# State-space stage of a hybrid decoder block: result channels on the partitions instead of tokens

## The chip, the cores and the metric

The kernel runs on one core of a Trainium2 chip. The metric is the device time of one execution in microseconds (us); the median of several runs counts, and lower is better. TensorE (PE, with its weight loads as PEld), VectorE (DVE), ScalarE (ACT), GpSimd (POOL) and the DMA queues (SP issues most of them) each work through a list of instructions of their own, in order, and wait for each other through semaphores.

## The reference

One layer of a decoder trunk over 512 tokens of width 1024, in float32. One projection of the normalised input feeds three token mixers: a sparse attention (DSA), a second attention with compressed, selected and window keys (NSA), and a Mamba-2 state-space mixer (SSD). Gated, the three results go through an output projection and a feed-forward layer. What the change touches is the SSD mixer, in chunks of 128 tokens (c: chunk, g: group of 8 heads, h: head, p: one of 64 channels of a head):

```python
y_diag = jnp.einsum('bcijg,bcijgh,bcjgh,bcjghp->bcighp', cb, lmat, dtc, xs)
states = jnp.einsum('bcjgn,bcjgh,bcjghp->bcghpn', bm, decay_states * dtc, xs)
...
y_off = jnp.einsum('bcign,bcghpn,bcigh->bcighp', cm, h_in, jnp.exp(a_cum))
y = y_diag + y_off + xs * d_skip.reshape(SSD_GROUPS, SSD_HPG)[:, :, None]
y = y.reshape(bsz, seq, SSD_INNER)
y = rms_norm(y * jax.nn.silu(z.astype(jnp.float32)), norm_g)
```

`cb` is C times B transposed, `lmat` the lower-triangular decay between two tokens of a chunk, `h_in` the state carried into a chunk. `x`, `z`, B, C and the step sizes come from the projection, x, B and C after a causal convolution of width 4 and a silu.

## The kernel before, in words

**Two generators.** `main` runs the mixers one after the other: the DSA index and attention, then `ssd`, then the NSA attention. `filler` runs the dense work: all input projections, the gates (`do_mg`) and, in `branches`, the three branch projections, the output projection and the feed-forward layer. Each `yield` of `main` gives a number of nanoseconds, scaled by a ratio (R3 = 0.5 for `ssd`); `filler` is advanced until it has emitted as much. A scheduler then orders the instructions of each engine by its own estimate of when they are ready, with priorities, so the order on an engine is not the order of emission. Where `main` needs a projection it yields its name (`x0`, `z0`) and the filler is advanced until it is done; in `branches` the filler waits in turn for marks of the NSA attention (`nsa0`, `nsah`, `nsaq0`, `nsaq1`, `nsa`), since its branch is computed last, its final quarter of tokens in `b2`.

**Projections.** A product of two float32 operands of full precision is made of three products of halves (`mm3`, lines 455 to 457: hi·hi, hi·lo, lo·hi). `proj_tok` has tokens on the output partitions (the input stationary, weights moving) and `proj_ch` has channels there (weights stationary). Weights arrive as `wraw` by DMA on SP and are split into `whi` on ACT (line 172) and `wlo` on DVE or POOL (line 174).

**What feeds the stage.** `do_z` (line 721) projects z with `proj_tok`, makes silu(z) times two from a tanh (lines 724, 725) and stores it token by token in `xz_d`. `do_x` and `conv` (lines 771, 831) project x, B and C with `proj_ch`, run the convolution on DVE and the silu, transpose the result on PE (line 848) and store x token by token in `xz_d`, B and C in `bct_d`.

**The stage** (`ssd`, line 1262) has 16 units, one for each group g and chunk c, in the order (0,0), (1,0), (0,1), (1,1) and so on, then groups 2 and 3. `stage1` loads B, C (`bcx`, line 1273) and the running sums of the decay, broadcast to all partitions (`E`, line 1275), two units ahead; `load_xz` (line 1282) loads x and z. `stage2` makes C·B (`cbm`, line 1289), masks E on POOL (line 1290), takes exponentials on ACT (line 1293), multiplies with `cbm` on DVE (line 1300) and scales x on POOL by the step (`xt`, line 1295), by step and decay (`xw`, line 1298) and by D (line 1302). `stage3` multiplies C with the carried state (line 1311, output `po`), scales it by exp(a_cum) on DVE (line 1313), adds D·x on POOL (line 1314), makes the chunk's state (line 1318) and updates the carried one (lines 1323, 1324). Then come eight y products, one per head (line 1330): E stationary, 64 columns of `xt` moving, tokens on the output partitions. The sum is multiplied with z (lines 1334, 1335), squared and summed by row on ACT (line 1336), transposed by four PE transposes (line 1341, emitted in the unit after), scaled by the gain of the norm in four ACT evictions (line 1344) and stored in `yc_d` (line 1345). At the end the row sums give the norm's factor (`rst`, line 1378), stored in `rs_d`. `load_y` (line 811) loads `yc_d` for the branch and splits it into halves.

Of the kernel before, what the change touches and what calls it, by code (L numbers as in the profile page):

```python
# [41 lines left out]
def build_kernel(ctx, tc, A, out):  # L42
# [35 lines left out]
    xz_d = scratch("xz_d", [2 * S, 2048])  # L78
# [136 lines left out]
    def plan_order(item):  # L215
# [5 lines left out]
        elif kind == "z":  # L221
            P["z", k] = plan_tok(w_in, D_IN, [(C_Z + k * 512, 512)])
# [95 lines left out]
    dskip = cp.tile([128, 32], F32, name="dskip")  # L318
    CL = {}

    def const_load():
# [20 lines left out]
        put(dskip, A["ssd_d"], 32)  # L342
# [348 lines left out]
    def filler():  # L691
# [119 lines left out]
    def load_y(yp, br, kk):  # L811
# [8 lines left out]
        act.activation(h_, yr, AF.Copy)  # L820
        dve.tensor_tensor(l_, yr, f(h_), op=ALU.subtract)
# [7 lines left out]


    def conv(m, p):
# [10 lines left out]
        if m >= 16:  # L842
            nc.sync.dma_start(bct_d[(m - 16) * 128:(m - 15) * 128], so)
        if m < 20:
            def tr():
# [5 lines left out]
                if m < 16:  # L851
                    nc.sync.dma_start(xz_d[:S, m * 128:m * 128 + 128].rearrange("(t p) c -> p t c", p=128), ev)
# [346 lines left out]
    def ssd_prelude():  # L1199
# [28 lines left out]
        for k in ("dth", "acm", "dw", "ea", "dec", "nac"):  # L1228
# [7 lines left out]
    def ssd_prelude2(sv, t, tri1, dta):  # L1236
# [10 lines left out]
        dve.scalar_tensor_tensor(sv["dw"], sv["dw"], 2.0, sv["dth"], op0=ALU.mult, op1=ALU.mult)  # L1247
        act.activation(sv["ea"], sv["acm"], AF.Exp)
        i_ = dve.tensor_scalar(sv["ea"], sv["ea"], 0.5, None, op0=ALU.mult)
        with tc.issue_after(getattr(i_, "ins", i_)):  # L1250
            dve.tensor_scalar(dskip, dskip, 0.5, None, op0=ALU.mult)
# [10 lines left out]
    def ssd(sv, ratio):  # L1262
        sp = popen("ssd", side="right")
        ssq = cp.tile([128, 4, 4], F32, name="ssq_y")
        col = lambda a, c, g: a[:, c * 32 + g * 8:c * 32 + g * 8 + 8]
        hst = {}

# [10 lines left out]
        def load_xz(u):  # L1278
            rows = slice(u.c * 128, u.c * 128 + 128)
            cols = slice(u.g * 512, u.g * 512 + 512)  # L1280
            xz = sp.tile([128, 2, 512], F32, name="xz", bufs=3)
            nc.sync.dma_start(xz, xz_d.rearrange("(k s) d -> s k d", k=2)[rows, :, cols])
            u.xs, u.zs = xz[:, 0], xz[:, 1]

        def stage2(u):
            g, c = u.g, u.c
            x3 = lambda a: a.rearrange("p (h d) -> p h d", d=64)
            cbm = ps("pv", [128, 512])[:, :128]
            pe.matmul(cbm, u.b[:, 0], u.b[:, 1], start=True, stop=True)
# [11 lines left out]
            u.xd = u.xs  # L1301
# [504 lines left out]
```

## Time and profile before

| | us |
|---|---|
| median of 3 runs | 1375.47 (1375.29 to 1377.54) |
| profiled execution, first to last instruction | 1374.2 |
| PE busy in it | 1352.5 |
| DVE busy | 1001.6 |
| ACT busy | 723.3 |
| POOL busy | 266.7 |
| first and last y product (line 1330) start at | 410.4 and 529.4 |

The times of the profile are those of one execution, and no other time is listed for it than its span, which is 1.3 us below the median of the runs. Busy time of PE counts overlapping matmuls once, up to a modelled end, so that a single matmul's duration is longer than the distance between two of them; where the text counts what a matmul costs, it takes the distance of starts. A float32 product that isn't split by `mm3` stands as two records.

### The profile page before, as it was taken

What the parts mean: (1) busy time and instruction counts of PE and PEld (TensorE: products, weight loads), DVE (VectorE), ACT (ScalarE), POOL (GpSimd) and SP (SyncE); (2) the same over time, 40 slices, a digit from 0 to 9 for tenths busy, and PEclk for the clock granted to TensorE, in tenths of its full rate; (3) what the DMA queues carried; (4) which work ended last, traced back from release to release, by engine and by line L of the source; (5) the groups of instructions that cost most, each with busy time, mean ns of one, the idle gap of its engine ahead of it and who ended that gap; (6) DMA issues with size and microseconds to landing.
All of it is one profiled execution on the core that took longest, in us unless ns stands there. A gap on an engine that the chain in (4) does not pass through costs nothing.

```text
span 1374.2 us, 19666 instructions
## 1 busy us (share of the span) xinstructions
PE 1352.5 (98%) x6875; PEld 1129.7 (82%) x6875; DVE 1001.6 (73%) x1968; ACT 723.3 (53%) x1434; POOL 266.7 (19%) x230
## 2 busy tenths in 40 slices
PE   9999999999998999999999999999999999999998
PEld 7888888888886767888888888887989888888887
DVE  6499987989877576876676888987745666767741
ACT  5455345676766675566666566553224344443430
POOL 2425111111027783200000001114101201102000
PEclk9999999999999999999999999999999999999999
DMA  6436555554467886635345454546535665846531
GB/s 196 119 91 156 176 162 157 131 140 119 112 215 237 245 252 182 170 104 146 104 115 154 126 147 115 150 138 191 180 112 165 128 167 124 183 113 132 153 119 50
DMA packets 222592, 205.34 MB, mean 149 GB/s; under 512 B 15369, under 2 KB 169885, under 8 KB 222494
## 3 DMA queue, kind: packets, MB, share of 16 engines
q1 hardware_dynamic: 206524, 180.49, 44.8%
q0 software_dynamic: 15232, 20.98, 8.1%
q10 hardware_dynamic: 738, 2.63, 0.5%
q8 instruction: 54, 0.88, 0.3%
q14 instruction: 44, 0.36, 0.1%
HBM read 167.56 MB, written 36.51 MB: 148 GB/s over the span
## 4 chain that ended last, share of the span: by engine, by line
PE 90%; DVE 3%; POOL 2%; DMA 2%; issue 2%; ACT 1%; SPq 0%; DVEq 0%; POOLq 0%; ACTq 0%
PE pj L455 21%; PE pj L456 21%; PE pj L457 21%; PE sc L457 3%; PE sc L455 3%; PE sc L456 3%; PE pT L944 3%; PE sc L906 2%; PE sc L905 2%; PE pv L956 2%; PE pv L957 2%; DMA E<-ac_d 1%; PE pF L944 1%; PE sc L1330 1%; POOL t L1314 1%
## 5 line engine op out<-in xcount | busy, mean ns | idle before, releaser
L172 ACT ACTIVATE whi<-wraw 128x1024 fp32r<-128x1024 f32 (+2 forms) x190 | 198.4, 1047 | 222.4 <-PE pj L456 109.9
L174 DVE TENSOR_TENSOR wlo<-wraw,whi 128x1024 fp32r<-128x1024 f32 (+1 forms) x176 | 226.0, 1287 | 95.4 <-ACT whi L172 93.8
L455 PE MATMUL pj<-hTh,whi 128*128 128x512 f32 x384 | 153.8, 401 | 0.0
L457 PE MATMUL pj<-hTh,wlo 128*128 128x512 f32 x384 | 153.1, 399 | 0.0
L456 PE MATMUL pj<-hTl,whi 128*128 128x512 f32 x384 | 152.8, 398 | 0.0
L914 ACT ACTIVATE p<-p,nb,rs 128x256 f32<-128x256 f32 (+3 forms) x192 | 123.2, 645 | 38.7 <-DVE nb L912 38.6
L455 PE MATMUL pj<-whi,hTh 128*128 128x512 f32 (+2 forms) x336 | 132.0, 393 | 2.6 <-DVE v_s L556 2.2
L456 PE MATMUL pj<-wlo,hTh 128*128 128x512 f32 (+2 forms) x336 | 131.7, 392 | 0.0
L457 PE MATMUL pj<-whi,hTl 128*128 128x512 f32 (+2 forms) x336 | 131.1, 390 | 0.0
L455 PE MATMUL pj<-yh,whi 128*128 128x512 f32 (+1 forms) x288 | 105.9, 374 | 1.9 <-DVE rtok L1535 0.8
L456 PE MATMUL pj<-yl,whi 128*128 128x512 f32 (+1 forms) x288 | 107.4, 373 | 0.0
L457 PE MATMUL pj<-yh,wlo 128*128 128x512 f32 (+1 forms) x288 | 106.6, 370 | 0.0
L456 PE MATMUL pj<-h2l,whi 128*128 128x512 f32 (+1 forms) x256 | 96.3, 376 | 0.0
L457 PE MATMUL pj<-h2h,wlo 128*128 128x512 f32 (+1 forms) x256 | 96.2, 376 | 0.0
L455 PE MATMUL pj<-h2h,whi 128*128 128x512 f32 (+1 forms) x256 | 96.1, 376 | 0.0
L1000 POOL DMA_DIRECT2D qu<-q_d x32 | 23.5, 735 | 330.8 <-PE sc L906 165.4
L457 PEld LDWEIGHTS pj<-hTh,wlo 128*128 128x128 f32 x384 | 72.2, 188 | 14.6 <-issue 0.7
L456 PEld LDWEIGHTS pj<-hTl,whi 128*128 128x128 f32 x384 | 72.3, 188 | 13.5 <-issue 0.7
L455 PEld LDWEIGHTS pj<-hTh,whi 128*128 128x128 f32 x384 | 72.3, 188 | 13.4 <-issue 0.5
L948 ACT ACTIVATE pth<-pT 128x512 fp32r<-128x512 f32 x95 | 55.0, 593 | 49.7 <-PE pT L944 48.1
L455 PEld LDWEIGHTS pj<-whi,hTh 128*128 128x128 f32 x336 | 64.0, 190 | 15.6 <-DVE v_s L556 2.5
L457 PEld LDWEIGHTS pj<-whi,hTl 128*128 128x128 f32 x336 | 63.8, 190 | 12.0 <-issue 0.5
(403 smaller groups left out, 3265.0 us busy)
## 6 DMA issues: line engine op xcount, KB each, us to landing
wraw<-in_w_in_dram SPq DMA_DIRECT2D x84, 512.0 KB, 4.1
wraw<-in_w_ff_dram SPq DMA_DIRECT2D x58, 512.0 KB, 4.3
qd<-in_w_ff_dram POOLq DMA_DIRECT2D x18, 512.0 KB, 5.9
gld<-g_d SPq DMA_DIRECT2D x35, 256.0 KB, 2.7
q_d<-qev SPq DMA_DIRECT2D x64, 128.0 KB, 2.5
qu<-q_d POOLq DMA_DIRECT2D x32, 256.0 KB, 3.8
E<-ac_d SPq DMA_DIRECT2D x16, 512.0 KB, 6.0
xz<-xz_d SPq DMA_DIRECT2D x16, 512.0 KB, 6.0
```

Source lines behind the costliest of these rows:

```text
L172: act.activation(hi[:, :m], r[:, :m], AF.Copy)
L174: (pool if i in LOWP else dve).tensor_tensor(lo[:, :m], r[:, :m], f(hi[:, :m]), op=ALU.subtract)
L455: pe.matmul(o, lh, rh, start=first, stop=False)
L456: pe.matmul(o, lh, rl, start=False, stop=False)
L457: pe.matmul(o, ll, rh, start=False, stop=last)
L905: pe.matmul(s_[:, h % w, :n], u.q[h], kh[:, :n], start=True, stop=False)
L906: pe.matmul(s_[:, h % w, :n], u.q[h], kl[:, :n], start=False, stop=True)
L914: act.activation(u.p[h][:, :n], u.p[h][:, :n], AF.Exp, bias=u.nb[:, h:h + 1], scale=rs8[:, u.b, u.h0 + h:u.h0 + h + 1], accum_out=u.sm[:, ...
L944: pe.transpose(pt[:, h], u.p[h][:, kb * 128:kb * 128 + 128], ident)
L948: act.activation(ph, ptf, AF.Copy)
L956: pe.matmul(o, vk, ph0, start=st, stop=False)
L957: pe.matmul(o, vk, pl0, start=False, stop=en)
```

## The change

z is projected with `proj_ch`, so that its channels are on the partitions, and stored in `xzt_d`, a new scratch tensor in which each unit's block lies by channel. `conv` also scales x by D/2 on ACT and stores it there (`put_t`), so D·x is no longer made in the stage; x itself stays token by token in `x_d`. In the stage `xt` and the carried state become the stationary operands and E and C the moving ones: each y product has 64 stationary columns and 128 moving ones, and writes output partitions 0 to 63 for even heads and 64 to 127 for odd ones, so a unit's result has channels on the partitions. `po` becomes four products. exp(a_cum) is taken from E for each unit on ACT, before E is masked, in two instructions. The transposes and their evictions are gone, the result is stored as it is, and the norm's gain goes into `load_y`. The squares are summed over channel blocks on POOL, and over partitions by four PE products with one column at the end. `mm` gives the stage's matmuls an order among themselves that the scheduler keeps. Lines after the first hunk are moved by one to some twenty lines: `mm3` is at 458 to 460, the stage's matmuls all at 1283 (inside `mm`), the attention's at 961, 973 and 974.

```diff
-    xz_d = scratch("xz_d", [2 * S, 2048])
+    x_d = scratch("x_d", [S, 2048])
+    xzt_d = scratch("xzt_d", [2, 4, NB, 128, 4, 128])
...
-            P["z", k] = plan_tok(w_in, D_IN, [(C_Z + k * 512, 512)])
+            P["z", k] = [(m, plan_ch(w_in, D_IN, C_Z + 128 * m)) for m in range(4 * k, 4 * k + 4)]
...
-        put(dskip, A["ssd_d"], 32)
+        for e in range(2):
+            nc.sync.dma_start(dcol[64 * e:64 * e + 64], dram(A["ssd_d"], e, [[0, 64], [2, 16]]))
+        dve.tensor_scalar(dcol, dcol, 0.5, None, op0=ALU.mult)
...
-            def cbz(t, p):
+            for m, i in P["z", o]:
+                p = ps("pj", [128, 512])
+                yield from proj_ch(i, hh, hl, p)
+                run_later()
...
-                nc.sync.dma_start(xz_d[S + t * 128:S + t * 128 + 128, o * 512:o * 512 + 512], zo)
-            yield from proj_tok(P["z", o], hTh, hTl, cbz)
+                put_t(1, m, zo)
...
+        if br[0] == "c":
+            gk = gcol[:, kk:kk + 1]
+            act.activation(h_, yr, AF.Copy, scale=gk)
+            dve.scalar_tensor_tensor(l_, yr, gk, f(h_), op0=ALU.mult, op1=ALU.subtract)
...
+    def put_t(w, m, src):
+        dst = xzt_d[w, m // 4].rearrange("c p k i -> p k c i")[:, m % 4]
+        nc.sync.dma_start(dst, src.rearrange("p (c i) -> p c i", c=NB))
...
+        else:
+            act.activation(acc, so, AF.Copy, scale=dcol[:, m:m + 1])
+            put_t(0, m, acc)
...
+        def mm(*a):
+            i_ = pe.matmul(*a, start=True, stop=True)
+            tc.stamp_issue_order_token(getattr(i_, "ins", i_), "ssd")
...
+            u.xs = sp.tile([128, 512], F32, name="xs", bufs=2)
+            nc.sync.dma_start(u.xs, x_d[u.c * 128:u.c * 128 + 128, u.g * 512:u.g * 512 + 512])
             xz = sp.tile([128, 2, 512], F32, name="xz", bufs=3)
-            nc.sync.dma_start(xz, xz_d.rearrange("(k s) d -> s k d", k=2)[rows, :, cols])
-            u.xs, u.zs = xz[:, 0], xz[:, 1]
+            nc.sync.dma_start(xz, xzt_d[:, u.g, u.c].rearrange("w p k i -> p w (k i)"))
+            u.xd, u.zs = xz[:, 0], xz[:, 1]
...
+            if c:
+                u.ea = sp.tile([128, 4, 128], F32, name="eab", bufs=2)
+                E2 = u.E.rearrange("p (k e) i -> p k e i", e=2)
+                for e in range(2):
+                    r = slice(64 * e, 64 * e + 64)
+                    act.activation(u.ea[r], E2[r, :, e], AF.Exp)
...
-            pool.tensor_tensor(x3(u.xd), x3(u.xs), bc(dskip[:, g * 8:g * 8 + 8][:, :, None], [128, 8, 64]), op=ALU.mult)
...
-                pe.matmul(po, u.b[:, 1], hst[g], start=True, stop=True)
+                for k in range(4):
+                    mm(po[:, 128 * k:128 * k + 128], hst[g][:, 128 * k:128 * k + 128], u.b[:, 1])
...
-            if TR:
-                TR.pop()()
-                yield ratio * 436
             for h in range(8):
-                pe.matmul(py[:, h * 64:h * 64 + 64], u.E[:, h], u.xt[:, h * 64:h * 64 + 64], start=True, stop=True)
-                if h % 4 == 3:
-                    yield ratio * 856
-            yv = sp.tile([128, 512], F32, name="yv", bufs=2)
+                e, cs = h % 2, slice(128 * (h // 2), 128 * (h // 2) + 128)
+                mm(py[64 * e:64 * e + 64, cs], u.xt[:, h * 64:h * 64 + 64], u.E[:, h])
+            yield ratio * 1300
+            yv = sp.tile([128, 512], F32, name="yv", bufs=1)
             dve.tensor_tensor(yv, py, t1 if c else u.xd, op=ALU.add)
-            dve.tensor_tensor(yv, yv, u.zs, op=ALU.mult)
-            act.activation(u.zs, yv, AF.Square, accum_out=ssq[:, c, g:g + 1])
+            dve.tensor_tensor(u.zs, yv, u.zs, op=ALU.mult)
+            nc.sync.dma_start(yc_d[g, c], u.zs)
+            act.activation(yv, u.zs, AF.Square)
...
-                    pe.transpose(pt[:, k], yv[:, k * 128:k * 128 + 128], ident)
...
-                    act.activation(ev[:, k], pt[:, k], AF.Copy, scale=gcol[:, 4 * g + k:4 * g + k + 1])
-                nc.sync.dma_start(yc_d[g, c], ev.rearrange("p k q -> p (k q)"))
...
+                pool.tensor_tensor(lo, lo, hi, op=ALU.add)
+                pool.tensor_tensor(sq4[c], sq4[c], lo, op=ALU.add)
...
+            pe.matmul(pq[:, c:c + 1], sk, mhalf[:, 0:1], start=True, stop=True)
```

More of the change, by code (lines that the diff above doesn't have):

```diff
@@ L317, in build_kernel @@
     alog = cp.tile([128, 32], F32, name="alog")
-    dskip = cp.tile([128, 32], F32, name="dskip")
+    dcol = cp.tile([128, 16], F32, name="dcol")
     CL = {}
@@ L851, in tr @@
                 if m < 16:
-                    nc.sync.dma_start(xz_d[:S, m * 128:m * 128 + 128].rearrange("(t p) c -> p t c", p=128), ev)
+                    nc.sync.dma_start(x_d[:, m * 128:m * 128 + 128].rearrange("(t p) c -> p t c", p=128), ev)
                 else:
@@ L1227, in ssd_prelude @@
         sv = {}
-        for k in ("dth", "acm", "dw", "ea", "dec", "nac"):
+        for k in ("dth", "acm", "dw", "dec", "nac"):
             sv[k] = cp.tile(n, F32, name="sv_" + k)
@@ L1246, in ssd_prelude2 @@
         act.activation(sv["dw"], t["b"], AF.Exp)
[L1247 to L1251, printed above, removed]
+        dve.tensor_tensor(sv["dw"], sv["dw"], sv["dth"], op=ALU.mult)
         yield 700.0
@@ L1278, in load_xz @@
         def load_xz(u):
-            rows = slice(u.c * 128, u.c * 128 + 128)
-            cols = slice(u.g * 512, u.g * 512 + 512)
+            u.xs = sp.tile([128, 512], F32, name="xs", bufs=2)
+            nc.sync.dma_start(u.xs, x_d[u.c * 128:u.c * 128 + 128, u.g * 512:u.g * 512 + 512])
             xz = sp.tile([128, 2, 512], F32, name="xz", bufs=3)
-            nc.sync.dma_start(xz, xz_d.rearrange("(k s) d -> s k d", k=2)[rows, :, cols])
-            u.xs, u.zs = xz[:, 0], xz[:, 1]
+            nc.sync.dma_start(xz, xzt_d[:, u.g, u.c].rearrange("w p k i -> p w (k i)"))
+            u.xd, u.zs = xz[:, 0], xz[:, 1]
         def stage2(u):
             g, c = u.g, u.c
-            x3 = lambda a: a.rearrange("p (h d) -> p h d", d=64)
             cbm = ps("pv", [128, 512])[:, :128]
-            pe.matmul(cbm, u.b[:, 0], u.b[:, 1], start=True, stop=True)
+            mm(cbm, u.b[:, 0], u.b[:, 1])
+            if c:
[4 more added lines that the diff above has]
+                    act.activation(u.ea[r], E2[r, :, e], AF.Exp)
             pool.affine_select(out=u.E, in_=u.E, compare_op=ALU.is_ge, fill=NEG, base=0,
@@ L1310, in stage3 @@
                 po = ps("sc", [128, 512])
[L1311 to L1313 removed]
+                for k in range(4):
+                    mm(po[:, 128 * k:128 * k + 128], hst[g][:, 128 * k:128 * k + 128], u.b[:, 1])
+                t1 = u.ea.rearrange("p k i -> p (k i)")
+                dve.tensor_tensor(t1, po, t1, op=ALU.mult)
                 pool.tensor_tensor(t1, t1, u.xd, op=ALU.add)
[L1315 removed]
+                yield ratio * 960
             if c < 3:
                 pst = ps("pT", [128, 512])
[L1318 removed]
+                mm(pst, u.b[:, 2], u.xw)
                 if c == 0:
@@ L1371, in ssd @@
             yield from stage3(us[i])
-        TR.pop()()
-        yield ratio * 436
-        sst = sp.tile([128, 4], F32, name="sst")
-        dve.tensor_reduce(sst, ssq, AX.X, ALU.add)
-        dve.tensor_scalar(sst, sst, 1.0 / 2048, 4 * EPS, op0=ALU.mult, op1=ALU.add)
-        rst = sp.tile([128, 4], F32, name="rst")
+        pq = ps("pT", [128, 512])
+        for c in range(NB):
+            sk = sq4[c][:, 0:128]
+            dve.tensor_tensor(sk, sk, sq4[c][:, 128:256], op=ALU.add)
+            pe.matmul(pq[:, c:c + 1], sk, mhalf[:, 0:1], start=True, stop=True)
+        sst, rst = sq4[2][:, 128:132], sq4[3][:, 128:132]
+        dve.tensor_scalar(sst, pq[:, 0:4], -2.0 / 2048, 4 * EPS, op0=ALU.mult, op1=ALU.add)
         pool.tensor_tensor(rst, sst, mhalf[:, :4], op=ALU.pow)
@@ L1380, in ssd @@
         pe.transpose(pt[:4, 0], rst, ident)
[L1381 removed]
+        rt = sq4[1][0:4, 128:256]
         act.activation(rt, pt[:4, 0], AF.Copy)
```

27 lines of the change are left out of this document (10 added, 17 removed).

## The prediction

> **What bounds the kernel now.** I read the page first, then the waits of PE, then the busy time by stretches of the span, then the chain of waits inside the state-space stage, and last single stretches of the timeline. The page and the waits:
>
> ```profile
> span 1374.2 us, 19666 instructions
> PE 1352.5 (98%) x6875; PEld 1129.7 (82%) x6875; DVE 1001.6 (73%) x1968; ACT 723.3 (53%) x1434; POOL 266.7 (19%) x230
> ```
> ```profile
> PE pT L1318 <- DVE hst L1324: 2.7, 2, 2.5
> PE pv L1289 <- DVE E L1300: 2.5, 2, 1.8
> PE pT L1341 <- DVE yv L1335: 2.5, 3, 1.1
> ...
> PE pT L1341 <- ACT yev L1344: 2.2, 3, 1.1
> ```
>
> PE is busy 1352.5 of 1374.2 us, so work that leaves PE is time, and so is a PE wait. The four waits shown (9.9 us) all belong to the stage that is changed; 4.7 of them are waits of the y transposes (L1341). The stretches show where PE has slack:
>
> ```profile
> core 0: us, PE busy (x) PEld busy (x) DVE busy (x) ACT busy (x) POOL busy (x), PEclk, DMA share, GB/s
> ...
> 200.00:300.00 100.00, 100.00 (x509) 83.65 (x508) 85.49 (x193) 66.72 (x140) 13.18 (x17) 1.00 0.56 144
> 300.00:350.00 50.00, 50.00 (x266) 42.17 (x265) 44.14 (x102) 33.50 (x69) 5.36 (x7) 1.00 0.46 122
> ...
> 400.00:450.00 50.00, 43.94 (x231) 33.85 (x230) 37.32 (x42) 33.56 (x93) 37.82 (x31) 0.98 0.81 265
> 450.00:500.00 50.00, 49.35 (x283) 39.33 (x282) 31.70 (x38) 34.76 (x106) 39.27 (x36) 0.98 0.78 238
> 500.00:540.00 40.00, 36.19 (x200) 28.42 (x199) 24.66 (x31) 26.61 (x75) 21.07 (x18) 1.00 0.71 204
> ```
>
> From 200 to 350 us PE never rests. Between 400 and 540, the state-space stage, it is idle 10.5 us, every other engine is 60 to 80% busy, and DMA is at 0.81 with 265 GB/s. What a record costs on PE there is read from the chain of waits, which counts start to start (a 128x128 by 512-column product in one pass takes 0.23; a float32 product stands as two records):
>
> ```profile
> 454.40 0.24 PE pj L457
> 454.64 0.84 PE sc L1330 x8
> 455.48 0.45 PE pT L1341 x4
> ```
> ```profile
> L1330 PE MATMUL sc<-xt,E 128*128 128x64 f32 x256 | 32.4, 267 | 0.2 <-DVE t L1313 0.2
> L1341 PE MATMUL pT<-ident,yv 128*128 128x128 f32 x64 | 11.5, 279 | 4.6 <-DVE yv L1335 2.5 <-ACT yev L1344 2.2
> ```
>
> A y record (E stationary, 128 columns loaded for 64 moving ones) takes 0.105; a transpose, with 128 moving columns, 0.1125.
>
> **The change part by part.** PE's order at the same unit of work (cbm, state product, y products), before:
>
> ```order
> L457 MATMUL pj<-hTh,wlo 128x512
> L1289 MATMUL pv<-bcx 128x128
> L848 MATMUL pF<-ident,craw 128x128 x4
> L1330 MATMUL sc<-xt,E 128x64 x4
> L1311 MATMUL sc<-hst,bcx 128x512
> L1341 MATMUL pT<-ident,yv 128x128 x4
> L1330 MATMUL sc<-xt,E 128x64 x4
> L1318 MATMUL pT<-xw,bcx 128x512
> L455 MATMUL pj<-hTh,whi 128x512
> ```
>
> And after, same place, same engine (all stage products now stand at line 1283):
>
> ```order
> L459 MATMUL pj<-hTl,whi 128x512
> L1283 MATMUL pv<-bcx 128x128
> L1283 MATMUL sc<-bcx,hst 128x128 x4
> L1283 MATMUL pT<-xw,bcx 128x512
> L1283 MATMUL sc<-E,xt 64x128 x8
> L460 MATMUL pj<-hTh,wlo 128x512
> ```
>
> The transposes are gone, the y products stand in one block of eight, and their outputs have 64 rows.
>
> *Transposes.* 16 groups of four at 0.45: -7.2. Their 64 ACT evictions go too.
>
> *y products.* 256 records at 0.105 (32 groups of 0.84) are 26.9 now. The new record loads 64 columns and moves 128, and successive products write output rows 0-63 and 64-127 from different column halves of the array. No product of before uses the upper half, so overlap of two halves can't be read here. The one group with 64 stationary columns:
>
> ```profile
> 106.05 0.39 PE L455 MATMUL pj<-whi,hTh 128*128 128x512 f32 x1
> 106.28 0.39 PE L456 MATMUL pj<-wlo,hTh 128*128 128x512 f32 x1
> 106.59 2.08 PE L655 MATMUL pT<-cmpw,xc 128*64 128x64 f32 x32
> 108.60 0.50 PE L457 MATMUL pj<-whi,hTl 128*128 128x512 f32 x1
> 108.94 0.40 PE L873 MATMUL sc<-ikT,iqT 128*128 128x512 f32 x1
> ```
> ```profile
> L655 PE MATMUL pT<-cmpw,xc x64: 222/222/270, 106.6 to 137.5; 128*64 128x64 f32 x64
> ```
>
> 32 records run in 2.08, the last alone lasting 0.222, so one takes (2.08-0.222)/31 = 0.060. The ends are 0.060 (the halves stream side by side and the short loads set the pace) and 0.1125 (they queue, the transpose's price for 128 moving columns). I choose 0.060, because L655 is nearest in what is loaded and alternating halves share neither stationary columns nor output rows; it is a choice, not a reading. 256 x 0.060 = 15.4: -11.5 (other end: +1.9). The Trainium skill, TensorEngine Tiling (Array Packing), section Key Properties, says that tiles of a divided array load and multiply in parallel; by it the sum stays as I have it; no run here shows it yet.
>
> *Going into 64 columns and back.* From 106.28 to 108.94 are 2.66 us. Two wide products at 0.23 and 32 records at 0.060 make 2.38; the two crossings cost 0.28. Sixteen blocks: +4.5.
>
> *Carried-state product.* One 512-wide product of two records becomes four of 128 columns; eight records at 0.105 to 0.1125 are 0.84 to 0.90, against
>
> ```profile
> 449.19 1.71 PE sc L1311 x2
> ...
> 456.76 0.91 PE sc L1311 x2
> ```
>
> 0.91 where nothing delays it: 0 (-0.8 to 0). Four products with one column for the sum of squares add 8 x 0.105: +0.8.
>
> *z by channels.* The same 384 products with stationary and moving swapped; weights come in 512-byte rows, as those of x do at 300-350, where PE is 50.00 of 50 busy. 0, covered by buffered weights.
>
> *D.x early.* 16 ACT scalings of about 0.6 (as L962's row below) and 16 stores of 256 KB on SP's queue, in stretches where ACT is 66.72 of 100 busy: 0. The two broken loads of ssd_d in 4-byte pieces stand ahead of early weight loads on SP, and the DVE scaling behind them ahead of a hTl split that PE needs: +0.5 (0 to 2.7, the largest total in the waits above).
>
> *POOL.* The D multiply goes, the running sum of squares comes:
>
> ```profile
> L1302 POOL TENSOR_TENSOR xz<-xz,dskip 128x512 f32<-128x512 f32 x16 | 20.1, 1258 | 0.5
> ```
>
> 20.1 leave; 28 adds of half the width at half of 1.258 (estimate) are 17.6. 0. On ACT two exponentials per unit replace four evictions: even.
>
> *Waits in the stage.* The 4.7 of the transposes can go. But the block is now rigid: its first product, once late, holds back the other sixteen and all projections queued behind. I give half back: -2.5 (-8 to +8).
>
> *The end of the attention that follows.* Between the stage's first and last product the order now has 478 projection rows instead of 240, so the following attention starts later against the projections that cover it. Its end on PE, before (cph, pth, ptl are its last probabilities):
>
> ```order
> L1108 MATMUL pv<-cph,vz 128x128 x4
> L956 MATMUL pv<-pth,v_w_310 128x512
> L957 MATMUL pv<-ptl,v_w_310 128x512
> L956 MATMUL pv<-pth,v_s_308 128x512
> L957 MATMUL pv<-ptl,v_s_308 128x512
> L455 MATMUL pj<-yh,whi 128x512
> L456 MATMUL pj<-yl,whi 128x512
> ```
>
> And after:
>
> ```order
> L961 MATMUL pF<-ident,p 128x128
> L961 MATMUL pT<-ident,p 128x128
> L1125 MATMUL pv<-cph,vz 128x128 x4
> L961 MATMUL pT<-ident,p 128x128 x2
> L973 MATMUL pv<-pth,v_w_311 128x512
> L458 MATMUL pj<-yh_9980,whi 128x256 x2
> L974 MATMUL pv<-ptl,v_w_311 128x512
> L459 MATMUL pj<-yl_9981,whi 128x256
> ```
>
> Before, the last value product has 36 wide and 96 half-wide rows behind it that don't need it; now the 84 rows behind it all do. And between the last scores and their transposes stand 24 half-wide rows, not 125 wide ones. The chain to be covered:
>
> ```profile
> 926.26 0.49 ACT L914 ACTIVATE p<-p,nb,rs 128x128 f32<-128x128 f32 x1 [2.18 <-DVE nb L912]
> ...
> 928.10 0.19 ACT L914 ACTIVATION_READ_ACCUMULATOR p<-p,nb,rs 128x1 f32 x1
> 928.79 0.40 ACT L926 ACTIVATE p<-p,rc 128x128 f32<-128x128 f32 x1 [0.50 <-DVE rc L922]
> ...
> 956.88 0.59 ACT L962 ACTIVATE yt<-pv 64x512 f32<-64x512 f32 x1 [1.10 <-PE pv L957]
> ```
> ```profile
> 957.98 0.84 DVE L967 TENSOR_TENSOR yr<-pv,yt 64x256 f32<-64x256 f32 x2
> 959.30 0.43 DVE L969 TENSOR_TENSOR yl<-yr,yh 128x256 fp32r<-128x256 f32 x1 [0.48 <-ACT yh L968]
> ```
>
> One softmax runs from 926.26 to 929.19, two interleaved some 6 us with the score maxima; PE has about 3.4 there (24 x 0.12, two wide products): 2.6 uncovered. From 956.88 to 959.73 the last result is put together: 2.8 with nothing beside it. Together 5.4; I take +5 (0 to +9).
>
> **Sum.** -7.2 - 11.5 + 4.5 + 0 + 0.8 + 0.5 - 2.5 + 5 = -10.4. The profiled span of 1374.2 becomes 1363.8; the median of the runs, 1375.47, lies 1.3 above the span, so 1365.1.
>
> **Rivals.** *The halves queue one behind the other* (ends slower). Each y record then costs 0.1125, 28.8 in all: 13.4 more, 1378.5. It decides from about 0.10 per record on, where the crossings and the attention's end have eaten the transposes. For it: in the rows above a product starts only when the one before it has streamed. Against: none of those pairs used different columns.
>
> *The second half's weights load only once the first half streams its last record.* Per product one load of 64 columns (half of 0.105, an estimate) and one stream of 0.105, 0.16 per two records: 20.5 in all, 1370.2. The Trainium skill, TensorE: Matmul & The Clock Gate, Part 3 (What overlaps and what doesn't), lets loads run beside matmuls only where their row groups differ, which these two halves' don't; but in this trace PEld (82% busy) runs beside PE in full-array streams, so I give it less.
>
> *DMA becomes the stage's bound* (slower too):
>
> ```profile
> E<-ac_d SPq DMA_DIRECT2D x16, 512.0 KB, 6.0
> xz<-xz_d SPq DMA_DIRECT2D x16, 512.0 KB, 6.0
> ```
>
> A unit now also loads 256 KB of x alone, and the x projections beside it store 256 KB more per result: by my count 2.7 MB per unit against 1.9. With some 22 projection rows a unit has about 8.4 us of PE work, so it needs 320 GB/s; 0.81 of share gave 265. At 265 a unit lasts 10.2, and eight units lose 14: 1379. It decides below about 280 GB/s. Against: 265/0.81 = 327 is there to be had, and no PE wait above names a DMA.
>
> **Chances and range.** Forecast 0.47, late weights 0.18, queued halves 0.22, DMA 0.13. The forecast's own range is 1356 to 1373 (waits and the attention's end at their bounds, not all at once); 1356 to 1380 leaves out under 2 in 10. A measurement tells about 0.2% (2.7 us) from no change. Forecast and late weights give nearly all of faster (0.62); queued halves and DMA split into same (0.16) and slower (0.22).
>
> **What would show it.** y records starting 0.06 apart, not 0.08 or 0.11; no L1341 rows; about 0.28 around each block; PE waits in the stage near 8 us; a wait of 2 to 3 us of the last branch products for the attention's last yl. A y record at 0.10 or more, or PE waits over 20 us in the stage, would make the prediction wrong.

## The result, and the profile after

The changed kernel takes 1394.09 us (median of 4 runs, 1392.76 to 1396.1); the kernel before took 1375.84 beside it. The ratio is 1.0130 (95% interval 1.0115 to 1.0144): 18 us slower, where 10 us faster was forecast, and above the upper end of the range. All medians and ratios in this document are of fast executions: of the seven of experiment 10 one was slow (1896.8 us at a granted clock of 0.65) and is left out. The profiled span grew from 1374.2 to 1394.4 us. The page after:

```profile
span 1394.4 us, 19715 instructions
...
PE 1348.1 (97%) x6891; PEld 1121.8 (80%) x6891; DVE 999.7 (72%) x1970; ACT 729.6 (52%) x1393; POOL 277.7 (20%) x242
```

PE is busy 4.4 us less than before, in a span that is 20.2 longer: the loss is idle time. Its largest piece lies nowhere near the state-space stage. PE's waits in the first 100 us:

```profile
PE pT L427 <- DVE hTl L438: 16.3, 1, 16.3
```

One wait of 16.3 us: the transposes of the first input wait for its split on DVE. Stretches from 20 to 50 us, after:

```profile
core 0: us, PE busy (x) PEld busy (x) DVE busy (x) ACT busy (x) POOL busy (x), PEclk, DMA share, GB/s
20.00:30.00 10.00, 4.35 (x25) 3.64 (x23) 0.88 (x1) 2.61 (x7) 0.00 (x0) 0.86 0.05 0
30.00:40.00 10.00, 0.00 (x0) 0.00 (x0) 0.12 (x2) 0.00 (x0) 0.00 (x0) 0.50 0.20 63
40.00:50.00 10.00, 9.30 (x41) 8.48 (x42) 5.98 (x11) 3.94 (x10) 0.00 (x0) 0.79 0.28 98
```

And before:

```profile
20.00:30.00 10.00, 10.00 (x57) 9.08 (x56) 5.58 (x10) 5.51 (x14) 0.00 (x0) 1.00 0.51 154
30.00:40.00 10.00, 10.00 (x52) 8.71 (x52) 7.89 (x12) 6.66 (x17) 3.98 (x3) 1.00 0.46 125
40.00:50.00 10.00, 10.00 (x55) 8.37 (x55) 2.55 (x7) 4.00 (x11) 0.00 (x0) 1.00 0.18 54
```

After, the transfers stand at 0 GB/s from 20 to 30 us, and from 30 to 40 every engine stands still but for 0.12 us of DVE. When PE returns at 40.7 us its granted clock is still down: 0.50 until 44.2, then 1.00, so 0.79 in the stretch from 40 to 50, with 41 records instead of 55. The chain of waits and DVE's timeline name what was waited for:

```profile
16.83 0.66 SPq L344
17.54 22.24 DMA dcol<-in_ssd_d_dram
```
```profile
39.88 0.17 DVE L345 TENSOR_SCALAR dcol<-dcol 128x16 f32<-128x16 f32 x1 [19.00 <-DMA dcol<-in_ssd_d_dram]
39.96 1.28 DVE L438 TENSOR_TENSOR hTl<-pT,hTh 128x512 fp32r<-128x512 f32 x2
```

The second of the two loads of `ssd_d` in 4-byte elements lands 22.2 us after its issue; DVE's halving of `dcol` waits 19 us for it, and the split `hTl` stands right behind. The stage starts at 418.1 us instead of 403.6, 14.5 later, although 24 projection rows fewer (5.5 us at 0.23) stand ahead of it: some 20 us are lost at the start.

The stage itself did what it was to do. One unit's block of y products on PE's timeline, with the wide products around it:

```profile
573.27 0.39 PE L460 MATMUL pj<-hTh,wlo 128*128 128x512 f32 x1
573.59 1.09 PE L1283 MATMUL sc<-E,xt 128*64 128x128 f32 x16
574.61 0.50 PE L458 MATMUL pj<-hTh,whi 128*128 128x512 f32 x1
574.95 0.40 PE L459 MATMUL pj<-hTl,whi 128*128 128x512 f32 x1
```

Sixteen records fill 1.02 us. In the trace they start in pairs 6 to 7 ns apart, the next pair 102 to 103 ns later (once in a block 153 to 154), so a pair takes 0.109 and a record 0.0545. From 573.27 to 574.95 are 1.68 us; two wide products at 0.23 and 16 x 0.0545 make 1.33, which leaves 0.35 for the two crossings. PE's waits in the stage (`issue` is time for which the profile shows nothing waited for):

```profile
PE pv L1283 <- issue: 2.3, 1, 2.3
PE pF L617 <- DVE qev L621: 2.0, 2, 1.5
PE pj L458 <- DVE cacc L851: 2.0, 1, 2.0
PE pv L1283 <- PE sc L1283: 0.8, 1, 0.8
```

These are 7.1 us instead of 10.5, no transposes and no DMA among them. The rest of the loss lies behind the stage, in the NSA attention. PE's largest waits there (590 to 1010 us), after:

```profile
PE pj L458 <- ACT yh L985: 2.1, 1, 2.1
PE pF L961 <- DVE p L947: 1.9, 3, 1.0
PE pj L458 <- ACT yh L827: 1.3, 2, 0.9
PE sc L1058 <- DVE mx L924: 1.2, 1, 1.2
```

And before, in the same part (545 to 990 us), all there were:

```profile
PE pj L455 <- DVE rtok L1535: 0.8, 1, 0.8
PE pj L455 <- ACT yh L820: 0.7, 1, 0.7
PE pj L455 <- DVE gld L1535: 0.4, 1, 0.4
```

In all PE is idle there 13.6 us instead of 1.9, mostly waits for the attention's own softmax (`mx`, `p`, `yh` of line 985). The attention's first score is issued at 599 us instead of 546, when 1862 of the 3072 projection rows that stand ahead of the output projection are gone instead of 1639.

### The profile page after: what moved, and what is told of

It reads as the page before. It is cut to its first block, busy times and chain, and to the rows that moved or that the text cites. A ratio compares the mean times of both kernels' runs of the same rounds, so it can differ in the third digit from the quotient of the medians.

```text
span 1394.4 us, 19715 instructions
## 1 busy us (share of the span) xinstructions
PE 1348.1 (97%) x6891; PEld 1121.8 (80%) x6891; DVE 999.7 (72%) x1970; ACT 729.6 (52%) x1393; POOL 277.7 (20%) x242
## 4 chain that ended last, share of the span: by engine, by line
PE 78%; DVE 8%; DMA 7%; issue 3%; ACT 2%; POOL 1%; SPq 1%; DVEq 0%; ACTq 0%; POOLq 0%
PE pj L458 19%; PE pj L460 18%; PE pj L459 18%; PE sc L460 3%; PE sc L459 3%; PE sc L458 3%; PE pT L961 2%; DMA gld<-g_d 2%; DMA dcol<-in_ssd_d_dram 2%; PE sc L1283 2%; PE sc L923 1%; PE sc L922 1%; PE pv L973 1%; PE pv L974 1%; DVE wlo L175 1%
## 5 line engine op out<-in xcount | busy, mean ns | idle before, releaser
L458 PE MATMUL pj<-hTh,whi 128*128 128x512 f32 x512 | 204.1, 399 | 2.3 <-DVE cacc L851 2.0
L460 PE MATMUL pj<-hTh,wlo 128*128 128x512 f32 x512 | 203.1, 397 | 0.0
L459 PE MATMUL pj<-hTl,whi 128*128 128x512 f32 x512 | 202.5, 396 | 0.0
L460 PEld LDWEIGHTS pj<-hTh,wlo 128*128 128x128 f32 x512 | 96.7, 189 | 19.0 <-issue 0.2
L459 PEld LDWEIGHTS pj<-hTl,whi 128*128 128x128 f32 x512 | 96.7, 189 | 18.6 <-issue 0.2
L458 PE MATMUL pj<-whi,hTh 128*128 128x512 f32 (+2 forms) x208 | 81.7, 393 | 3.3 <-DVE v_s L559 2.2
L460 PE MATMUL pj<-whi,hTl 128*128 128x512 f32 (+2 forms) x208 | 80.7, 388 | 0.0
L459 PE MATMUL pj<-wlo,hTh 128*128 128x512 f32 (+2 forms) x208 | 80.4, 387 | 0.0
L966 DVE TENSOR_TENSOR ptl<-pT,pth 128x512 fp32r<-128x512 f32 x95 | 63.8, 680 | 6.2 <-ACT pth L965 6.0
L458 PEld LDWEIGHTS pj<-yh,whi 128*128 128x128 f32 x288 | 54.9, 192 | 15.0 <-ACT yh L985 2.5
```

Source lines behind the costliest of these rows:

```text
L458: pe.matmul(o, lh, rh, start=first, stop=False)
L459: pe.matmul(o, lh, rl, start=False, stop=False)
L460: pe.matmul(o, ll, rh, start=False, stop=last)
L966: dve.tensor_tensor(pl, ptf, f(ph), op=ALU.subtract)
```

## The experiments

Theory A: the two 4-byte loads cost the 20 us at the start. Theory B: the y products gain by the overlap of column halves. Theory C: the attention loses because too few projection rows are left beside its end. Against A stands that the hole would have come anyway; against B that a record is short by itself; against C another cause behind the stage, above all the token (the mark by which `mm` gives the stage's products their fixed order); beside them stands D, DMA as the stage's bound. "Idle" below is time in which PE has no record running; "behind the stage" runs from the last y product to 990 us (in the changed kernel, which is some 20 us later, from 590 to 1010).

**1. The D values as one contiguous row** (from here on called the row kernel)

```diff
+        wide("dsk", A["ssd_d"], 32)
         for e in range(2):
-            nc.sync.dma_start(dcol[64 * e:64 * e + 64], dram(A["ssd_d"], e, [[0, 64], [2, 16]]))
-        dve.tensor_scalar(dcol, dcol, 0.5, None, op0=ALU.mult)
+            r = slice(64 * e, 64 * e + 64)
+            dve.tensor_scalar(dcol[r], CL["dsk"][r].rearrange("p (m e) -> p m e", e=2)[:, :, e], 0.5, None, op0=ALU.mult)
```

> The D skip values come as one contiguous row with the other early constants and are spread to the 128 partitions by two strided VectorE instructions; the two loads of 4-byte elements are gone; all else as in the changed kernel. Theory A (those loads hold VectorE and so TensorE at the start, about 20 us in all: 16.35 us idle before 40.7 us and records at half clock until 54.9 us): TensorE's idle time in the first 100 us goes from 21.6 to about 5 us, the state-space stage starts near 405 us instead of 418 us, the time is about 1394 - 20 = 1374 us (1371 to 1378). Rival (the idle time is a wait for something else that was late anyway, or the time lost there comes back later): over 1385 us.

1377.93 us (1373.48 to 1380.59), ratio to before 1.0017 (1.0000 to 1.0033). Idle in the first 100 us is 5.2 us, the stage starts at 399.7, the span is 1373.5. The hole is gone:

```profile
20.00:30.00 10.00, 10.00 (x58) 9.10 (x57) 5.98 (x11) 6.01 (x17) 0.00 (x0) 1.00 0.51 157
30.00:40.00 10.00, 10.00 (x53) 8.66 (x52) 7.86 (x13) 6.12 (x13) 3.98 (x3) 1.00 0.46 125
```

A holds: by medians the loads cost 16 us. By spans it is 20.9, but 6.4 of these are PE busy for longer with the same 6891 records (1348.1 against 1341.7), and the mean granted clock of these two executions is 0.987 and 0.996; the return at half clock explains under 2 of the 6.4. The expectation's "half clock until 54.9 us" is a misreading: the clock was back at 44.2. But the kernel is now level with the one before, not 10 us faster, and 14.3 us of idle time still stand behind its stage.

**2. The kernel before with the two loads added**

```diff
+    dcol = cp.tile([128, 16], F32, name="dcol")
...
+        for e in range(2):
+            nc.sync.dma_start(dcol[64 * e:64 * e + 64], dram(A["ssd_d"], e, [[0, 64], [2, 16]]))
+        dve.tensor_scalar(dcol, dcol, 0.5, None, op0=ALU.mult)
```

> The kernel before, with nothing added but the two loads of 4-byte elements and the VectorE instruction that halves them, at the same place, the result used by nothing. Theory A (the loads are slow by themselves and stand ahead of the split of the first input on VectorE): the same hole of 14 to 17 us before 41 us and the same half clock behind it, about 1375.5 + 20 = 1395 us (1390 to 1399). Rival (the loads cost only beside the other edits): within 2 us of 1375.5 us.

1396.57 us, ratio 1.0159 (1.0144 to 1.0174), with the same wait:

```profile
PE pT L428 <- DVE hTl L439: 17.0, 1, 17.0
```

Two instructions that load 8 KB, and the halving behind them, slow the kernel before by 21 us. A is shown from both sides.

**3. The halving issued late**, everything else as in the changed kernel, the loads too:

```diff
-        dve.tensor_scalar(dcol, dcol, 0.5, None, op0=ALU.mult)
...
+        i_ = dve.scalar_tensor_tensor(so, th, 1.0, acc, op0=ALU.add, op1=ALU.mult)
...
+            if "dcol" not in CL:
+                CL["dcol"] = dcol
+                with tc.issue_after(getattr(i_, "ins", i_)):
+                    dve.tensor_scalar(dcol, dcol, 0.5, None, op0=ALU.mult)
             act.activation(acc, so, AF.Copy, scale=dcol[:, m:m + 1])
```

> The changed kernel with the two loads of 4-byte elements kept as they are; only the VectorE instruction that halves their result is issued later, behind the first convolution, where the values are first needed. Theory A1 (the loss at the start is VectorE's wait for the landing, in front of the first input's split): TensorE's idle time in the first 100 us falls from 21.6 to about 5 us and the time to that of the run with the contiguous row, about 1376 us (1370 to 1380). Rival A2 (the 2048 elements hold the transfers of the others, or SyncE's two issues of 0.66 us hold theirs, so the loads cost without anybody waiting for them): over 10 us idle in the first 100 us and over 1385 us.

1374.71 us, ratio 0.9987 (0.9971 to 1.0002). The time is what A1 expected, but not for its reason: idle in the first 100 us is 13.6 us, not 5, and the stage starts at 413.5. The edit moved the scheduler's order elsewhere too (2904 instead of 2952 rows gone at the attention's last score), and less idle time there (3.1 us in the stage, 6.0 behind it) made up for the start. A2 has the idle time right (over 10 us) and the time wrong (over 1385 us). DVE no longer waits for the loads, but something else does. The chain of waits and the stretches:

```profile
17.56 22.84 DMA wraw<-in_w_in_dram
```
```profile
20.00:30.00 10.00, 10.00 (x58) 9.09 (x57) 4.33 (x8) 4.04 (x11) 0.00 (x0) 1.00 0.05 0
30.00:40.00 10.00, 4.98 (x24) 4.10 (x22) 0.00 (x0) 0.00 (x0) 0.00 (x0) 0.99 0.30 101
```

The weights issued behind the loads land only after 22.8 us. So the loads do two things: DVE waits for them, and nothing behind them is moved meanwhile. This kernel still has the token, and yet only 9.1 us of idle time in and behind the stage, where the row kernel has 22.4; that bears on experiment 7.

**4. The two loads on GpSimd's queue**, otherwise as experiment 3:

```diff
-            nc.sync.dma_start(dcol[64 * e:64 * e + 64], dram(A["ssd_d"], e, [[0, 64], [2, 16]]))
+            pool.dma_start(dcol[64 * e:64 * e + 64], dram(A["ssd_d"], e, [[0, 64], [2, 16]]))
```

> As the run with the late halving, but GpSimd issues the two loads of 4-byte elements instead of SyncE, on its own DMA queue; the order of TensorE's instructions is the same. There the weights issued behind the two loads landed 22.8 us after their issue, and for some 17 us nothing else was moved. Theory Q (the two loads hold only what stands behind them in the same queue): the weights land 3 to 5 us after issue, TensorE's idle time in the first 100 us goes from 13.6 to about 5 us, the stage starts at about 400 us instead of 413.5, the time is about 1374.7 - 10 = 1364 us (1360 to 1369). Rival E (2048 single elements occupy the 16 DMA engines themselves, whatever the queue): the hole of 17 us in the moved bytes stays, 12 us or more idle in the first 100 us, within 3 us of 1374.7 us.

1387.39 us, ratio 1.0067 (1.0049 to 1.0085): slower still. GpSimd issues the loads at 2.0 us, so the hole moves ahead, in front of the input itself:

```profile
10.00:15.00 5.00, 0.00 (x0) 0.00 (x0) 0.00 (x0) 0.00 (x0) 0.00 (x0) 0.56 0.20 30
15.00:20.00 5.00, 0.00 (x0) 0.00 (x0) 0.00 (x0) 0.96 (x1) 2.10 (x1) 0.50 1.86 75
20.00:25.00 5.00, 0.00 (x0) 0.00 (x0) 0.00 (x0) 0.00 (x0) 0.00 (x0) 0.50 0.09 31
```

SyncE's transfers crawl at 30 to 75 GB/s on their own queue. Q falls, and E holds in its kind, that the loads hold up the transfers of other queues too; its time (within 3 us of 1374.7) is missed by 10 us, since it expected the hole to stay where it was. That it is the single elements is shown by the row kernel, which reads the same values as contiguous rows, repeated to the partitions too, without a hole. The Trainium skill, DMA: Bandwidth & Descriptors, section Issuing engines are not separate DMA queues, says that transfers of all issuing engines run on the same 16 DMA engines; this trace agrees. Its section Rules for kernel authors says that a last dimension that isn't contiguous becomes one descriptor per element. In these runs 2048 such elements took 17 to 22 us.

**5. The two loads at 252 us**, issued by SyncE behind the first convolution's store, otherwise as experiment 3:

```diff
-            nc.sync.dma_start(bct_d[(m - 16) * 128:(m - 15) * 128], so)
+            d_ = nc.sync.dma_start(bct_d[(m - 16) * 128:(m - 15) * 128], so)
+            if m == 16:
+                with tc.issue_after(getattr(d_, "ins", d_)):
+                    for e in range(2):
+                        nc.sync.dma_start(dcol[64 * e:64 * e + 64], dram(A["ssd_d"], e, [[0, 64], [2, 16]]))
```

> As the run with the late halving, but SyncE issues the two loads of 4-byte elements behind the first convolution's store, at about 230 us, where weights stand buffered ahead of TensorE; order of TensorE's instructions as there. Theory Q2 (the price of the loads is the place: a hole of 17 us in the queue costs nothing behind buffered weights, or little): the same hole of 15 to 18 us in the moved bytes, there, with under 6 us of TensorE idle beside it; idle in the first 100 us about 5 us; 1362 to 1370 us. Rival (the buffers hold less than 17 us of work): over 8 us of TensorE idle around 230 to 260 us and no gain, 1371 to 1378 us.

1371.07 us, ratio 0.9945 (0.9927 to 0.9964); idle in the first 100 us is 4.2. The loads make the same hole at the new place:

```profile
250.00:260.00 10.00, 10.00 (x51) 8.37 (x50) 8.19 (x20) 5.86 (x11) 0.76 (x1) 1.00 0.15 34
260.00:270.00 10.00, 10.00 (x59) 8.45 (x58) 9.74 (x22) 6.32 (x13) 1.03 (x1) 1.00 0.05 0
270.00:280.00 10.00, 7.08 (x35) 5.72 (x35) 3.38 (x8) 2.01 (x5) 1.47 (x2) 1.00 0.89 255
```

PE works on for some 20 us and then loses 2.9. Q2 holds in its kind: buffered weights cover most of the hole. The time is 1 us above its range.

**6. Column halves one after the other** (on the row kernel)

```diff
-            for h in range(8):
+            for h in (0, 2, 4, 6, 1, 3, 5, 7):
```

> As the run with the contiguous row, but the eight y products of a unit go through the heads 0, 2, 4, 6, 1, 3, 5, 7, so that all four of one column half are issued before those of the other; same instructions, same waits. Theory B (two neighbouring records overlap only because they are in different halves): the records stand 0.10 us or more apart but for one pair in a block, 256 x 0.05 = 13 us more TensorE time in the stage, so 8 to 14 us slower than the run with the contiguous row where TensorE is the bound of the stage. Rival (two records of one half overlap just as well, and the 54.5 ns is a record's own duration): no difference, within 1.5 us.

1381.83 us, ratio to before 1.0048 (1.0033 to 1.0063), 3.9 us above the row kernel by medians and 7.6 by spans. The y products by groups, the row kernel and then this one:

```profile
L1284 PE MATMUL sc<-E,xt 128*64 128x128 f32 x256 | 17.5, 279 | 0.0
```
```profile
L1284 PE MATMUL sc<-E,xt 128*64 128x128 f32 x256 | 25.9, 283 | 0.0
```

The products take 8.4 us more. In a block the first five records start 0.16 and then 0.109 us apart; the next starts 6 ns behind the fifth, six more follow mostly 52 to 57 ns apart, and the last four stand 0.109 apart again. These are two rows of eight, each with one step of 0.16 and then steps of 0.109, the second begun beside the fifth record of the first. (The trace doesn't name a record's half; the rows are read from the steps.) In experiment 1 both halves have the same steps and run side by side from the first record on. So a half has its own pace, 0.109 a record, and only records of different halves overlap: B holds for the products, and its rival falls. They needn't be neighbours in the order, though: four of each row of eight still run beside the other row, and so it is 8.4 us and not 13, for which I took every record for doubled. The whole kernel loses about half of the 8.4 us by medians and nine tenths by spans; B's 8 to 14 us are not reached by medians, and the interval just touches that of the row kernel.

**7. The token left off** (on the row kernel)

```diff
-            tc.stamp_issue_order_token(getattr(i_, "ins", i_), "ssd")
```

> As the run with the contiguous row, only the token that keeps the stage's products in one order taken away; GpSimd's four powers stay inside the stage. Rows gone at the last score 2904, at the last value product 2982 (with the token 2952 and 2988; with both edits 2804 and 2868). Theory C: a little less idle time behind the stage than the 14.3 us of the run with the contiguous row, 10 to 13 us, and about 1375 us (1370 to 1378). Rival (the token alone is the cause, by the waits of one product for the other in the stage): as fast as the run with both edits, 1367 us.

1363.77 us (1360.49 to 1364.11), ratio to before 0.9900 (0.9877 to 0.9922). It beats both kernels, and by far more than C expected (1370 to 1378 us; the rival's 1367 is nearer): idle in the stage goes from 8.1 to 1.6 us, behind it from 14.3 to 4.9. PE's waits in the stage (400 to 570 us), the row kernel and then this one:

```profile
PE pv L1284 <- issue: 2.9, 1, 2.9
PE pF L618 <- DVE qev L622: 2.4, 2, 1.4
PE pj L459 <- DVE cacc L852: 2.0, 1, 2.0
PE pj L459 <- ACT gth L791: 0.7, 1, 0.7
```
```profile
PE pT L1284 <- POOL xw L1322: 1.6, 1, 1.6
```

With the token the stage's last y product is issued at 554.5 us, without it at 536.4. Only part of the eight products now stand in one block (39 blocks instead of 16), so y costs 21.9 us start to start instead of 16.6 and `po` 15.6 instead of 10.8; the idle time saved is more. This is not the token's price by itself: experiment 3 has the token and little idle time in and behind the stage. What the token costs depends on the order that the scheduler makes around it.

**8. The kernel before with the token** on its `cbm`, `po`, state and y products:

```diff
+        def mm(*a):
+            i_ = pe.matmul(*a, start=True, stop=True)
+            tc.stamp_issue_order_token(getattr(i_, "ins", i_), "ssd")
...
-            pe.matmul(cbm, u.b[:, 0], u.b[:, 1], start=True, stop=True)
+            mm(cbm, u.b[:, 0], u.b[:, 1])
```

> The kernel before, its state-space products with the token that keeps them in one order, nothing else. Rows gone at the last score 2755 instead of 2718, at the last y product 1597 instead of 1577. Theory T (the token itself costs: with it a product that is not ready holds the ones behind it and rows stand between them; taking it out of the changed kernel gave 14 us): slower than before, by 5 to 14 us, 1380 to 1390 us. Rival (the token only hurts with the new stage, whose products wait for one another differently): within 2 us of 1376 us.

1384.61 us, ratio 1.0064 (1.0040 to 1.0088). The token costs 8.6 us there too, with the old products. Idle in the stage even falls (10.5 to 8.2 us); behind the stage it goes from 1.9 to 8.4. T holds, within its 5 to 14 us; what is priced here is again one order that the scheduler made.

**9 to 12. Order behind the stage.** GpSimd's four powers for the query norms (12 us) stand inside the stage in the changed kernel. Four kernels move the order: the powers behind the first two query loads with the token kept (9); both edits (10); both, and the squares of all units but the first of each chunk left out of the sum, which leaves out most of the norm (11); the token off, powers in place, and the number that spaces the attention's steps changed (12).

```diff
-        for b in dict.fromkeys(b for b, _ in NORD):
-            pool.tensor_tensor(rs8[:, b, 16:32], ssn[:, b], mhalf[:, :16], op=ALU.pow)
...
+                        with tc.issue_after(HX["qu"]):
+                            pool.tensor_tensor(rs8[:, b_, 16:32], ssn[:, b_], mhalf[:, :16], op=ALU.pow)
```
```diff
-                pool.tensor_tensor(lo, lo, hi, op=ALU.add)
-                pool.tensor_tensor(sq4[c], sq4[c], lo, op=ALU.add)
```
```diff
-R0, R1, R2, R3 = 1000.0, 1.5, 2.5, 0.5
+R0, R1, R2, R3 = 1000.0, 1.5, 1.5, 0.5
```

> As the run with the contiguous row, with GpSimd's four powers issued behind the first two query loads; the token on the stage's products is kept. Theory C (what counts is how many projection rows are left for the attention's last part): the attention starts earlier (1810 rows gone instead of 1862), but its last score still has 2960 of 3072 behind it (2952 without this edit), so the idle time behind the stage stays near 14 us and the time near 1378 us (1374 to 1381). Rival (GpSimd's 12 us inside the stage are what costs): as fast as the run with both edits, 1367 us.

> As the run with the contiguous row, and two edits of order: GpSimd's four powers for the sparse attention's query norms are issued behind the first two of its query loads instead of inside the state-space stage, and the stage's products on TensorE no longer carry the token that keeps them in one order. Theory C (the attention starts too late behind the stage, so that the projection rows that should lie beside its last part run out: 1862 of 3072 are gone when its first score is issued, 1639 before the change): with 1766 gone at the first score and 2804 at the last score (before the change: 2718; changed: 2952), most of the 13.6 us of idle time behind the stage goes; about 1374 - 8 = 1366 us (1359 to 1369). Rival (the idle time there has another cause, or the stage loses as much without the token): within 2 us of the run with the contiguous row, or slower.

> As the run with both edits of order, but the gated squares of the units are not added up (only the first unit's are), which leaves out most of the normalization's sum: 24 GpSimd additions less behind the products. Rows gone at the last score 2717 and at the last value product 2844, those of the kernel before (2718 and 2844). Theory C: the idle time behind the stage falls to 2 to 3 us (5.6 us with both edits, 1.9 us before), and the time by 3 to 4 us to about 1363 us (1359 to 1366). Rival (the rest of that idle time has nothing to do with the place of the rows): as the run with both edits, 1367 us.

> As the run with the token taken away and GpSimd's powers left in place, with the number that spaces the sparse attention's steps in the planned order changed from 2.5 to 1.5: the state-space stage is issued just as there, only the rows beside the attention stand otherwise (2804 instead of 2904 rows gone at the last score, 2868 instead of 2982 at the last value product). Theory C (rows left for the last part decide): the 4.9 us of idle time behind the stage goes down to 2 to 3 us, 1361 us (1358 to 1363). Theory C2 (not the count at the end but how evenly the rows stand beside the attention decides, and fewer rows beside its middle uncover that): no gain or a loss, 1364 to 1370 us.

| kernel | rows gone at last score | idle behind the stage, us | median, us | ratio to before (95%) |
|---|---|---|---|---|
| before | 2718 | 1.9 | 1376 | 1 |
| row kernel | 2952 | 14.3 | 1377.93 | 1.0017 (1.0000 to 1.0033) |
| 9: powers late | 2960 | 10.8 | 1370.11 | 0.9949 (0.9933 to 0.9966) |
| 7: token off | 2904 | 4.9 | 1363.77 | 0.9900 (0.9877 to 0.9922) |
| 10: both | 2804 | 5.6 | 1366.67 | 0.9939 (0.9920 to 0.9958) |
| 11: both, sums out | 2717 | 10.7 | 1373.74 | 0.9975 (0.9963 to 0.9987) |
| 12: token off, spacing 1.5 | 2804 | 8.6 | 1367.09 | 0.9932 (0.9915 to 0.9950) |

C falls as I stated it, although 10 came out as it forecast (1359 to 1369). The idle time doesn't follow the rows gone at the last score: with the count of the kernel before (11) it is twice that of 7, and 12, with the stage of 7 and 100 rows more in hand, is slower. Experiment 9 gained where C said no change, and the powers are worth some 8 us with the token (9 against the row kernel), none without it (10 against 7). That the place of each row beside the softmaxes decides, as C2 has it, fits 12 (1367.1 in its 1364 to 1370) but is not shown by a run of its own; a simple number that tells it ahead was not found. PE's waits behind the stage in 7:

```profile
PE pj L459 <- ACT yh L828: 1.3, 2, 1.1
PE pj L459 <- ACT yh L986: 1.3, 1, 1.3
PE pj L459 <- DVE rtok L1552: 1.3, 1, 1.3
```

No softmax wait (`mx`, `p`) is left; the last `yh` still costs 1.3.

**13. x not stored and loaded by tokens** (on the row kernel). `x_d` is neither written nor read, and the products take the block by channels in its place, which leaves out the right x:

```diff
-            u.xs = sp.tile([128, 512], F32, name="xs", bufs=2)
-            nc.sync.dma_start(u.xs, x_d[u.c * 128:u.c * 128 + 128, u.g * 512:u.g * 512 + 512])
...
+            u.xs = u.xd
```

> As the run with the contiguous row, but the token-major copy of x is neither stored nor loaded (16 stores and 16 loads of 256 KB, 8.4 MB less); where the stage took x by tokens it takes the channel-major block of the same size, so the use of the right x in the states and the E products is left out. Theory D (the stage is held by transfers, 340 GB/s and a DMA share of 1.02 in its first 50 us): the stage gets shorter, 5 to 10 us faster than the run with the contiguous row. Rival (TensorE is fed in time anyway, 8.1 us idle in the stage of which the loads hold little): within 2 us of it.

1375.51 us, ratio 0.9995 (0.9982 to 1.0007), against 1.0017 (1.0000 to 1.0033) of the row kernel: 2.4 us by medians, and the two intervals overlap. The DMA share falls; the row kernel and then this one:

```profile
400.00:450.00 50.00, 48.01 (x282) 37.06 (x281) 42.65 (x49) 42.16 (x92) 34.86 (x32) 1.00 1.02 340
450.00:500.00 50.00, 47.55 (x303) 37.13 (x302) 30.13 (x35) 34.42 (x81) 33.56 (x33) 1.00 0.93 290
```
```profile
400.00:450.00 50.00, 47.00 (x278) 35.89 (x277) 39.53 (x48) 39.15 (x88) 32.41 (x31) 1.00 0.79 265
450.00:500.00 50.00, 45.63 (x265) 35.13 (x264) 30.43 (x37) 36.57 (x85) 29.60 (x30) 0.97 0.81 253
```

PE is no busier for it; over the whole of 400 to 550 us it is busy 142.6 us here and 142.6 in the row kernel. D falls: 8.4 MB less gives at most the 2.4 us, which this measurement hardly tells from nothing.

## Why the prediction was wrong, step by step

- **Transposes, -7.2: right.** No such rows are left; start to start they took 9.8 us, waits included.
- **y products, -11.5 at 0.060 a record: right in size, and in that the halves run side by side.** 0.0545 measured, and 6 shows that it is the halves. The reason for the number was wrong: I let the short loads set the pace, but within one half a record takes 0.109, near a transpose's 0.1125 for as many moving columns, while L655, with the same loads and half the moving columns, took 0.060. That half of 0.109 lies so near 0.060 is luck. The rule named beside it (the Trainium skill, TensorEngine Tiling (Array Packing), Key Properties) holds here. The rivals of queued halves (0.1125 a record) and of late second weights (0.08) fall; the weight loads of the two halves start 6 to 7 ns apart too, beside running records.
- **Crossings, +4.5: right in kind,** 0.35 a block instead of 0.28: 5.6.
- **Carried-state product 0:** 12.9 us start to start before, 10.8 in the row kernel, 15.6 in experiment 7. **Column sums +0.8:** 0.8.
- **z by channels, D·x early, POOL and ACT even, each 0:** not tried one by one. Busy time of POOL rose by 11.0 us and that of ACT by 6.3 in the changed kernel, so "even" was wrong for both, though neither is near full (20% and 52% of the span). Experiment 7, which holds them all, is 12.0 us shorter than before by spans, where the whole sum was -10.4.
- **The broken loads, +0.5 (0 to 2.7): this step failed first, and alone it takes the time out of the range** (without the loads it is 1377.93). I bounded them by the largest total in a list of waits of the kernel before, which holds no transfer of that kind. They cost 16 us here and 21 in the kernel before, by DVE's wait and by the standstill of all other transfers.
- **Waits in the stage, -2.5 (-8 to +8): -2.4 in the row kernel,** 10.5 to 8.1. I saw that the order was rigid, but priced it as waits inside the stage, and never priced what the token does to the order behind it, where its cost mostly shows. It is 14 us in the row kernel (1377.93 to 1363.77; 11.3 by spans) and 8.6 in the kernel before, and less where the order falls well (experiment 3). This is the second step that failed.
- **End of the attention, +5 (0 to +9): too small,** 12.4 us more idle time in the row kernel, 3.0 without the token. The last `yh` is one wait of 2.1, as forecast (2 to 3); the rest is spread over the attention's second half, not its last 10 us.
- **DMA as the bound:** falls (13). Up to 340 GB/s were moved in the stage, above the 320 that I said it would need.

Put together, by medians: the new products and layouts -12.7 us (7 against the kernel before), the token +14.2, the loads +16.2, in all +17.7 of the 18.3 measured. These are the steps of one chain of kernels, so they add up by construction and prove nothing more; the 0.6 is the kernel before, measured at 1376.5 beside 7 and at 1375.8 beside the changed kernel. The forecast of 1365.1 was near a kernel without the last two, 1363.8, but by luck in part. In the forecast PE's work falls by 13.4 us (transposes, y, crossings, column sums) and its waits rise by 3; in 7 PE is busy for 6.1 us less than before and idle for 5.9 less (15.8 of its span of 1362.2). And the order behind the stage moves the time by up to 10 us between the kernels of the table that have no token, which no term of the sum knew.

## What to carry to other kernels

Read the shape of every load that a change adds, however few bytes it has: here two that picked 4-byte elements held up all other transfers. Moving their consumer left 13.6 of 21.6 us of idle time at the start, and GpSimd's queue made it worse; a contiguous row with a strided read on an engine took the hole away, and a place behind buffered weights covered it but for 2.9 us. When a change also fixes an order, price that by itself, by taking the order off the changed kernel and by putting one on the kernel before, and expect the price to differ. And where a scheduler fills gaps with other work, an edit's price appears wherever that work runs out, so read the idle time of the whole span before you judge the stage that was edited.

## What the hardware showed that was not expected

- Two loads of 1024 elements of 4 bytes each, issued by SyncE, keep the transfers of the core at 0 GB/s for about 17 us. On the stretch from 13 to 45 us after the change, 40 slices of 0.8 us:

```profile
DMA  6877971000000000000000000000002469641089
GB/s 197 293 248 166 351 260 23 6 0 0 0 0 0 0 0 0 0 0 0 0 0 0 0 0 0 0 0 0 0 0 67 184 238 369 248 182 31 23 218 387
```

- The busy share of DMA reads near zero meanwhile (the upper row), and on GpSimd's queue it reads up to 1.86 at 75 GB/s (experiment 4): while single elements are moved, a low share is not room for more.
- After PE's 16 us of rest the granted clock stayed at 0.50 for 3.5 us beside returning work (40.7 to 44.2 us). The Trainium skill, TensorE: Matmul & The Clock Gate, Part 1, says that idle windows take the clock to half until a busy window has passed; the rows from 30 to 50 us agree (0.50, then 0.79).
- Products of two column halves start 6 to 7 ns apart and run side by side, each half at 0.109 us a record; going into 64 columns and back costs 0.35 us a block.
